# A row softmax on one core: the exponentials in a loop over a ring of 12 groups, broadcast multiplications on two engines, and one DMA queue for loads and stores

## The chip, the cores and the metric

The kernel runs on one core of one Trainium2 chip. The metric is the device time of one execution in microseconds (us), as the median of several runs. A profile is one execution more, taken by the hardware profiler, with a time of its own.

The engines that matter here are VectorE (DVE in the profile), ScalarE (ACT), GpSimd (POOL), SyncE (SP, which computes nothing and issues transfers) and the core's 16 DMA engines, which move data between the chip's memory (HBM) and the on-chip memory of 128 partitions (SBUF).

## The reference: what is computed

The input is 16 x 1024 = 16,384 rows of 512 numbers in float32. Each row is replaced by its softmax:

```python
x_max = np.max(x, axis=-1, keepdims=True)
exp_x = np.exp(x - x_max)
return (exp_x / np.sum(exp_x, axis=-1, keepdims=True)).astype(np.float32)
```

33.55 MB are read from HBM and 33.55 MB are written.

## The kernel before

**Tiles.** A chunk is 128 partitions x 16 rows x 512 numbers, which is 4 MiB; there are 8 chunks, and each is one load and one store. Partition p holds 16 consecutive rows, so that its part of a chunk is one piece of 32 KiB in HBM and in SBUF. The buffer `held` has room for 6 chunks; chunk 6 takes the place of chunk 0 and chunk 7 that of chunk 1. Everything is computed in place. The engines work on groups of 8 rows per partition, two groups to a chunk, 16 groups in all.

**One group.** `rowmax` (L86) is one VectorE reduction over 128 x 8 x 512 that gives the 8 negated row maxima (L88). `exps` (L90) is 8 ScalarE activations of 128 x 512, one for each row, with the negated maximum as bias and the row's sum as a second output (L93). `scale` (L102) is one VectorE reciprocal of the 8 sums (L104) and 8 VectorE multiplications of 128 x 512 by one number for each partition (L106).

**Order.** The main loop (L116 to L123) goes through the groups: maxima of group g, exponentials of group g, then scaling of group g-1. So VectorE alternates between a reduction and the scaling of the group before. The stores stand in the loop behind the groups that `STORE_BEHIND` names; the last ones follow it.

**Queues.** All 8 loads are issued by SyncE (L71). The first of them stands ahead of the barrier at the program's start (`loads_at_the_head`, L27), five follow at once, and loads 6 and 7 wait until stores 0 and 1 have landed, whose places they take. All 8 stores are issued by ScalarE (L74), between its activations. So loads and stores are in two DMA queues, q1 and q10 in the profile. Waits between engines are set by the framework from what each instruction reads and writes.

Of the kernel before, what the change touches and what calls it, by code (L numbers as in the profile page):

```python
# [1 line left out]

# [4 lines left out]

F32 = mybir.dt.float32
EXP = mybir.ActivationFunctionType.Exp
AX = mybir.AxisListType.X  # L10


CHUNK = 16
CHUNKS = 8
PLACES = 6
GROUP = 8

STORE_BEHIND = [1, 1, 1, 1, 0, 0, 0, 0]

LOAD_AFTER = {0: 6, 1: 7}  # L20


AT_HEAD = {mybir.EngineType.SP: 1}

def loads_at_the_head(nc):  # L27

    main, body = nc.main_func.blocks[0], nc.main_func.blocks[1]
    for engine, count in AT_HEAD.items():  # L30
        loads = [
            i
            for i in body.instructions
            if i.engine == engine and type(i).__name__ == "InstDMACopy"
        ][:count]
        barrier = next(
            n
            for n, i in enumerate(main.instructions)
            if i.engine == engine and type(i).__name__ == "InstDrain"
        )  # L40
        for load in loads:
            body.instructions.remove(load)
        main.instructions[barrier:barrier] = loads


@with_exitstack
def kernel(
    ctx: ExitStack,
    tc: tile.TileContext,
    x: bass.AP,  # L50
    out: bass.AP,
):
    nc = tc.nc
    nc.at_finalize(loads_at_the_head)
    P = nc.NUM_PARTITIONS

    x_rows = x.flatten_outer_dims().rearrange("(c p r) d -> c p r d", p=P, r=CHUNK)
    out_rows = out.flatten_outer_dims().rearrange("(c p r) d -> c p r d", p=P, r=CHUNK)
    n, _, _, d = x_rows.shape
    assert n == CHUNKS  # L60

    data = ctx.enter_context(tc.tile_pool(name="data", bufs=1))
    stats = ctx.enter_context(tc.tile_pool(name="stats", bufs=6))
    held = data.tile([P, PLACES * CHUNK, d], F32, name="held")

    def place(k):
        at = (k % PLACES) * CHUNK
        return held[:, at : at + CHUNK, :]

    def load(k):  # L70
        nc.sync.dma_start(out=place(k), in_=x_rows[k])  # L71

    def store(k):
        nc.scalar.dma_start(out=out_rows[k], in_=place(k))  # L74
        if k in LOAD_AFTER:
            load(LOAD_AFTER[k])

    per = CHUNK // GROUP
    groups = CHUNKS * per
    shift, sums = [None] * groups, [None] * groups  # L80

    def rows(g):
        at = (g % per) * GROUP
        return place(g // per)[:, at : at + GROUP, :]

    def rowmax(g):  # L86
        shift[g] = stats.tile([P, GROUP], F32, name="shift", tag="shift")
        nc.vector.reduce_max(out=shift[g], in_=rows(g), axis=AX, negate=True)  # L88

    def exps(g):  # L90
        sums[g] = stats.tile([P, GROUP], F32, name="sums", tag="sums")
        for r in range(GROUP):
            nc.scalar.activation(  # L93
                out=rows(g)[:, r, :],
                in_=rows(g)[:, r, :],
                func=EXP,
                bias=shift[g][:, r : r + 1],
                scale=1.0,
                accum_out=sums[g][:, r : r + 1],
            )  # L100

    def scale(g):  # L102
        recip = stats.tile([P, GROUP], F32, name="recip", tag="recip")
        nc.vector.reciprocal(out=recip, in_=sums[g])  # L104
        for r in range(GROUP):
            nc.vector.tensor_scalar_mul(  # L106
                out=rows(g)[:, r, :],
                in0=rows(g)[:, r, :],
                scalar1=recip[:, r : r + 1],
            )  # L110

    with tc.manual_schedule():
        for k in range(PLACES):
            load(k)
        stored = 0
        for g in range(groups):  # L116
            rowmax(g)
            exps(g)
            if g:
                scale(g - 1)  # L120
            if stored < CHUNKS and g > (stored + 1) * per - 1 + STORE_BEHIND[stored]:
                store(stored)
                stored += 1  # L123
        scale(groups - 1)
        while stored < CHUNKS:
            store(stored)
            stored += 1


# [1 line left out]
_INS = ['x']  # L131
_OUTS = [((16, 1024, 512), 'float32')]


# [23 lines left out]
```

## Time and profile before

| what | value |
|---|---|
| median of 3 runs | 161.6 us (161.31 to 162.15) |
| the profiled execution, its own time | 161.69 us |
| its span (first to last instruction) | 159.9 us |
| moved through DMA over the span | 67.1 MB, 420 GB/s |
| HBM read, written | 33.55 MB, 33.55 MB |

The profile's page has six parts: busy time by engine; the span in 40 equal slices, with the busy share of each engine and of the DMA engines in tenths; the DMA queues; the chain of work that ended last; the costliest groups of instructions, with the idle time ahead of them and what ended it; and the DMA issues. Further views are cut from the same trace: busy time and DMA rate in chosen stretches of the span, who waited for whom, and single instructions in order of time. The DMA views rest on one record for each packet that a DMA engine moved, with its start, its duration and its queue.

The span is 1.79 us shorter than the profiled execution's own time.

### The profile page before, as it was taken

The numbers are of one execution on the slowest core, as the hardware profiler recorded it, in microseconds if no ns is written. First come the engines' busy times: TensorE is split into PE (matmuls) and PEld (weight loads), VectorE is DVE, ScalarE is ACT, GpSimd is POOL, SyncE is SP. The second block draws the span as 40 slices with busy tenths as digits, with TensorE's granted clock in tenths as the row PEclk, the third lists the DMA queues.
The fourth block names the chain that finished last, engine by engine and source line by source line (L and its number), as shares of the span: only waits on it lengthen the run. The fifth ranks groups of instructions, "written<-read, shape, count | busy, mean of one in ns | idle before, by whom it ended". The sixth has DMA issues, their size and how long they took to land.

```text
span 159.9 us, 496 instructions
## 1 busy us (share of the span) xinstructions
DVE 123.5 (77%) x160; ACT 93.2 (58%) x257; POOL 0.2 (0%) x4
## 2 busy tenths in 40 slices
DVE  0008969999999999999999999999999997620000
ACT  0003799495959585867777685959594959300000
POOL 0000000000000000000000000000000000000000
DMA  8999999999999999999999999999999999999993
GB/s 270 459 443 402 451 459 402 426 469 410 402 393 393 500 412 402 467 434 410 426 459 410 418 484 404 402 500 410 402 426 484 393 410 500 402 402 500 410 402 148
DMA packets 2307, 67.13 MB, mean 420 GB/s; under 512 B 256, under 2 KB 256, under 8 KB 256
## 3 DMA queue, kind: packets, MB, share of 16 engines
q1 hardware_dynamic: 1152, 33.55, 49.5%
q10 hardware_dynamic: 1152, 33.55, 48.6%
q14 instruction: 3, 0.02, 0.0%
HBM read 33.55 MB, written 33.55 MB: 420 GB/s over the span
## 4 chain that ended last, share of the span: by engine, by line
DMA 48%; DVE 32%; ACT 8%; issue 1%; DVEq 0%; SPq 0%; ACTq 0%
DMA held<-in_x_dram 30%; DVE shift L88 19%; DMA out_dram<-held 18%; DVE held L106 12%; ACT held L93 8%; DVE recip L104 1%; DVEq L153 0%; SPq L71 0%; ACTq L93 0%
## 5 line engine op out<-in xcount | busy, mean ns | idle before, releaser
L93 ACT ACTIVATE held<-held,shift 128x512 f32<-128x512 f32 x128 | 90.5, 708 | 31.5 <-DVE shift L88 21.3
L88 DVE TENSOR_REDUCE shift<-held 128x8 f32<-128x4096 f32 x16 | 70.5, 4415 | 12.7 <-DMA held<-in_x_dram 12.7
L106 DVE TENSOR_SCALAR held<-held,recip 128x512 f32<-128x512 f32 x128 | 52.1, 482 | 0.6
L93 ACT ACTIVATION_READ_ACCUMULATOR held<-held,shift 128x1 f32 x128 | 23.9, 187 | 0.0
L93 ACT ACT_TABLE_LOAD x1 | 1.3, 1283 | 12.6 <-DMA held<-in_x_dram 12.6
L104 DVE RECIPROCAL recip<-sums 128x8 f32<-128x8 f32 x16 | 3.1, 196 | 4.0 <-ACT held L93 4.0
L142 POOL MEMSET const-bfloat16-1.0<- 128x1 bf16 x1 | 0.1, 101 | 0.0
L142 POOL MEMSET const-uint8-127<- 128x1 uint8 x1 | 0.1, 101 | 0.0
L142 POOL MEMSET const-float32-0.0<- 128x1 f32 x1 | 0.1, 98 | 0.2 <-issue 0.2
L142 POOL MEMSET const-float32-1.0<- 128x1 f32 x1 | 0.1, 98 | 0.0
## 6 DMA issues: line engine op xcount, KB each, us to landing
held<-in_x_dram SPq DMA_DIRECT2D x8, 4096.0 KB, 35.4
out_dram<-held ACTq DMA_DIRECT2D x8, 4096.0 KB, 28.4
```

Source lines behind the costliest of these rows:

```text
L88: nc.vector.reduce_max(out=shift[g], in_=rows(g), axis=AX, negate=True)
L93: nc.scalar.activation(out=rows(g)[:, r, :], in_=rows(g)[:, r, :], func=EXP, bias=shift[g][:, r : r + 1], scale=1.0, accum_out=sums[g][:, ...
L104: nc.vector.reciprocal(out=recip, in_=sums[g])
L106: nc.vector.tensor_scalar_mul(out=rows(g)[:, r, :], in0=rows(g)[:, r, :], scalar1=recip[:, r : r + 1],)
L142: nc = _bacc.Bacc("TRN2", target_bir_lowering=False, num_devices=1)
```

## The change

**Ring.** The buffer `ring` has 12 groups of 8 rows, the same bytes as 6 chunks, and is placed by hand with the statistics (`stat`: the negated maximum of a row, overwritten by its sum; `recip`). Tiles and pools are gone, and each wait is written out with a semaphore. Loads and stores still have 16 rows (two groups) and 4 MiB each, and partition p still holds 16 consecutive rows.

**ScalarE.** The 128 activations become a loop of 16 turns with 8 activations each, whose addresses are worked out in registers from `g % RING`. A turn waits for one group's maxima and signals when its 8 activations are done. ScalarE's function table is loaded ahead of the loop. It issues no DMA any more.

**VectorE.** Its order is written out in `SEQUENCE`: M is a reduction over one group, MM one over two groups, D a reciprocal and a multiplication on VectorE, P a reciprocal on VectorE and the multiplication on GpSimd. A multiplication is one instruction over 128 x 4096, with the 8 reciprocals spread along the rows (`spread`), in place of 8 instructions over 128 x 512. Groups 0, 1, 3, 5, 7, 9, 11, 13, 14 and 15 are multiplied on VectorE, groups 2, 4, 6, 8, 10 and 12 on GpSimd.

**One queue.** SyncE issues loads and stores alike: loads 0 to 5 first, as before, then the transfers in the order of `ORDER`, then store 7. A store waits until both its groups are multiplied; loads 6 and 7 wait until stores 0 and 1 have landed. What stands behind a waiting transfer on SyncE waits too.

Instructions as built: VectorE goes from 16 reductions, 16 reciprocals and 128 multiplications to 10, 16 and 10; GpSimd gets 6 multiplications; SyncE goes from 8 transfers to 16; ScalarE's program goes from 128 activations to a loop body of 8.

The diff, cut to its core (`+` is the kernel after):

```diff
-CHUNK = 16
-CHUNKS = 8
-PLACES = 6
 GROUP = 8
-STORE_BEHIND = [1, 1, 1, 1, 0, 0, 0, 0]
-LOAD_AFTER = {0: 6, 1: 7}
+RING = 12
+LOADS = [2, 2, 2, 2, 2, 2, 2, 2]
+STORES = [2, 2, 2, 2, 2, 2, 2, 2]
+ORDER = """
+S0 S1 L6 L7 S2 S3 S4 S5 S6
+"""
+SEQUENCE = """
+M0 M1 M2 D0 M3 D1 MM4 P2 MM6 D3 P4 MM8 D5 P6 MM10 D7 P8 MM12 D9 P10 MM14 D11 P12 D13 D14
+D15
+"""
...
+    ring = sbuf("ring", RING * GROUP * d)
+    stat = sbuf("stat", RING * GROUP)
+    recip = sbuf("recip", RING * GROUP)
...
     def load(k):
-        nc.sync.dma_start(out=place(k), in_=x_rows[k])
+        g, n = LOAD_AT[k], LOADS[k]
+        return nc.sync.dma_start(out=rows(g, n), in_=in_dram(x_rows, g, n))
     def store(k):
-        nc.scalar.dma_start(out=out_rows[k], in_=place(k))
-        if k in LOAD_AFTER:
-            load(LOAD_AFTER[k])
+        g, n = STORE_AT[k], STORES[k]
+        return nc.sync.dma_start(out=in_dram(out_rows, g, n), in_=rows(g, n))
...
+    def spread(t):
+        return t.unsqueeze(2).to_broadcast([P, GROUP, d])
...
+    def rowmax(g, groups):
+        nc.vector.wait_ge(loaded[load_of(g)], 16)
+        nc.vector.reduce_max(
+            out=cols(stat, g, groups), in_=rows(g, groups), axis=AX, negate=True
+        ).then_inc(maxima, groups)
+    def exps():
+        with nc.Fori(0, GROUPS, 1, engines=(ACT,)) as g:
+            nc.scalar.wait_ge(maxima, 1).then_inc(maxima, -1)
+            row = nc.scalar.snap((g % RING) * GROUP)
+            for r in range(GROUP):
+                done = exp(ring[:, bass.ds((row + r) * d, d)], stat[:, bass.ds(row + r, 1)])
+            done.then_inc(summed, 1)
+    def scale(g, engine):
+        nc.vector.wait_ge(summed, g + 1)
+        nc.vector.reciprocal(out=cols(recip, g), in_=cols(stat, g)).then_inc(inverted, 1)
+        engine.wait_ge(inverted, g + 1)
+        engine.tensor_mul(
+            out=rows(g), in0=rows(g), in1=spread(cols(recip, g))
+        ).then_inc(scaled[store_of(g)], 1)
...
+    def store_scaled(k):
+        nc.sync.wait_ge(scaled[k], STORES[k])
+        store(k).then_inc(done_by(k), 16)
+    with tc.manual_schedule(engines={ACT, DVE, POOL, SP}):
+        nc.scalar.preload_act_table(EXP)
...
+            exps()
+            for work in SEQUENCE.split():
...
+                if kind in ("M", "MM"):
+                    rowmax(g, len(kind))
+                else:
+                    scale(g, nc.vector if kind == "D" else nc.gpsimd)
+            for transfer in ORDER.split():
+                k = int(transfer[1:])
+                if transfer[0] == "S":
+                    store_scaled(k)
+                else:
...
+                    nc.sync.wait_ge(stored[last], 16 * (last - since))
+                    load(k).then_inc(loaded[k], 16)
+            nc.sync.wait_ge(scaled[-1], STORES[-1])
+        store(len(STORES) - 1)
```

## The prediction, on record before the result was known

> **What bounds the kernel now.** I read the page's busy row, the row of the DMA share, the queue rows, and then the DMA rate in stretches of the span.
>
> ```profile
> DVE 123.5 (77%) x160; ACT 93.2 (58%) x257; POOL 0.2 (0%) x4
> ...
> DMA  8999999999999999999999999999999999999993
> ...
> q1 hardware_dynamic: 1152, 33.55, 49.5%
> q10 hardware_dynamic: 1152, 33.55, 48.6%
> q14 instruction: 3, 0.02, 0.0%
> ```
>
> No engine is near 100%, but the DMA row reads 9 from the second slice to the last but one, and the two queues together take 98% of all 16 DMA engines' span. The chain of waits names DVE for 32%, but only because it steps from a store to the multiplication that released it: the transfers have other work meanwhile.
>
> The next view is the stretches (columns: stretch, length, busy time of DVE, ACT and POOL, clock, DMA share, GB/s).
>
> ```profile
> 0.00:12.50 12.50, 0.00 (x0) 0.00 (x0) 0.20 (x4) 1.00 0.94 383
> 10.00:39.90 29.90, 25.80 (x27) 19.99 (x54) 0.00 (x0) 1.00 1.01 436
> 39.90:48.00 8.10, 8.06 (x12) 6.12 (x17) 0.00 (x0) 1.00 1.00 396
> 48.00:128.00 80.00, 79.44 (x105) 59.83 (x169) 0.00 (x0) 1.00 1.00 432
> 128.00:156.00 28.00, 10.20 (x19) 7.22 (x21) 0.00 (x0) 1.00 1.00 432
> 156.00:158.00 2.00, 0.00 (x0) 0.00 (x0) 0.00 (x0) 1.00 0.69 295
> 158.00:159.90 1.90, 0.00 (x0) 0.00 (x0) 0.00 (x0) 1.00 0.00 0
> ```
>
> Until 39.9 only loads move, from 48 to 128 both directions from two queues, from 128 on only stores. The rate is 432 to 436 GB/s in all three. So a direction alone is as fast as both together, and one queue as fast as two. At 432 GB/s the 67.11 MB need 155.35 us. The span's rest is losses: 12.5 x (1 - 383/432) = 1.42 at the start; 8.1 x (1 - 396/432) = 0.68 where the first store joins the loads; 2 x (1 - 295/432) = 0.63 and 1.90 at the end. 155.35 + 1.42 + 0.68 + 0.63 + 1.90 = 159.98, against a span of 159.9. **A kernel with these transfers can win a part of 4.6 us and no more; any gap in the transfers adds its length.** All that the change does to the computing engines costs or brings nothing until a store or a load is late.
>
> **The DMA order in the kernel after.** Loads 0 to 5, stores 0 and 1, loads 6 and 7, stores 2 to 7, one after the other. 4.194 MB at 432 GB/s is 9.71 us each, and with the first loss of 1.42 the sixth load ends at 1.42 + 6 x 9.71 = 59.7. The slots then start at: S0 59.7, S1 69.4, L6 79.1, L7 88.8, S2 98.5, S3 108.2, S4 117.9, S5 127.6, S6 137.3, S7 147.0, with the end at 156.7. A store must be issued about 2 us ahead of its slot: bytes first move in the stretch from 0.5 to 1.0 after the first issue, and SP saw a landed store about 0.4 us after its last packet (83.2 to 83.7); the rest is margin.
>
> L6 needs S0 landed: 69.4 plus these 2 us is 71, and S1 occupies the engines until 79.1. L7 needs S1 landed, 81, and L6 runs until 88.8. S2 to S6 stand behind L7 on SP, so SP can't issue them before 81; S2's slot is 98.5. So the two new waits in front of stores are covered as long as S1 is issued by 67. Before, the same two waits were on SP with stores flowing in the other queue, which now can't fill a gap.
>
> **VectorE's plan.** Prices come from the groups (line, engine, operation, count | busy, mean ns | idle before).
>
> ```profile
> L93 ACT ACTIVATE held<-held,shift 128x512 f32<-128x512 f32 x128 | 90.5, 708 | 31.5 <-DVE shift L88 21.3
> L88 DVE TENSOR_REDUCE shift<-held 128x8 f32<-128x4096 f32 x16 | 70.5, 4415 | 12.7 <-DMA held<-in_x_dram 12.7
> L106 DVE TENSOR_SCALAR held<-held,recip 128x512 f32<-128x512 f32 x128 | 52.1, 482 | 0.6
> L104 DVE RECIPROCAL recip<-sums 128x8 f32<-128x8 f32 x16 | 3.1, 196 | 4.0 <-ACT held L93 4.0
> ```
>
> - M: 4.36 (4415 ns less the overlap with the next instruction; the chain has 4.33), MM twice that.
> - D, the broadcast multiplication over 128 x 4096, is in no row. Below: 3.26, what the chain shows for 8 multiplications of 512. Above: two passes of the 4415 ns row, 8.8, if the spread operand needs a pass of its own. I take 4.4, the nearest row: one instruction over the same 4096 numbers.
> - P, the same on GpSimd, is in no row; its only rows are constants of 128x1 at 98 to 101 ns. Below 4.4; above three passes of 4415 ns, 13.2. I take two passes, 8.8.
> - A reciprocal with its wait 0.2. ACT's turn: 5.76 for 8 activations (the chain: 16 pieces, 5.76). The loop's registers, wait and branch are in no row: below, nothing; above, the longest ACT wait without a seen releaser ("issue" in the waits view, 10.2 us in 5, longest 2.3) in each turn, 8.1. I take 6.0.
>
> Load 0 lands at 12.5 as before. Then M0 to 16.9, M1 21.2, M2 26.1 (load 1 lands at 21.7), D0 30.7, M3 35.1, D1 39.7, MM4 48.4, MM6 57.3, D3 61.9, MM8 70.8, D5 75.4, MM10 84.3, D7 88.9, MM12 98.4 (it waits 0.5 for load 6), D9 103.0, MM14 111.9, D11 116.5, D13 121.3, D14 125.9, D15 130.5. GpSimd starts P2 at 48.6 and has it at 57.4, P4 70.9, P6 84.4, P8 97.9, P10 112.0, P12 125.5. Stores are ready, against the need 2 us ahead of their slots: S0 39.7 (57.7), S1 61.9 (67.4), S2 75.4 (96.5), S3 88.9 (106.2), S4 103.0 (115.9), S5 116.5 (125.6), S6 125.5 (135.3), S7 130.5 (145.0). **No slot runs empty.** The tightest is S1, by 5.5 us.
>
> Other prices in the same plan tell where gaps begin. D: S5 has 9.1 us to spare and eight D ahead of it, so D over 5.6. P: six in a row from 48.6 must be done by 135.3, P over 14.4. ACT: 16 turns from 16.9 and one D by 145.0, a turn over 7.7; the 8.1 of the upper bound would cost 16 x 0.4 = 6 us. So ACT's cover is 1.9 us a turn over the row, and the loop is costed at nothing. The multiplications saved on VectorE (52.1 us busy become 44) are hidden, too.
>
> **Port rule.** Before, GpSimd does nothing beside VectorE, so no row prices the two together. If a D and a P exclude each other and M doesn't mind, the same plan has D13 wait for P12, S7 ready at 139.1, still 6 us early; but gaps begin at P over 9.8 (from 48.6, six P, five D with their reciprocal at 4.8, and the last three D, 13.6, must be done by 145.0), and then grow by 6 us for each us of P. The Trainium skill speaks against the change here: "SBUF — State Buffer", section "Who interferes with whom", says that a VectorE instruction with two SBUF inputs and a GpSimd one that reads SBUF hold the shared port in turn, the second blocked until the first is done, and that reductions are free of it. No run here shows it. "GPSIMD Engine Reference", section "Performance versus the Vector engine", has 4497 ns for 2048 columns of a two-input add; an estimate from that page is 9.0 for P, by which the sum stays the same.
>
> **What goes.** q14 is instruction loading: three packets of 8 KB in the span, at 34.5, 58.4 and 98.6 by the packet records, each holding one DMA engine for 0.31 us. At the end, 13 of 16 engines finish between 157.3 and 157.8, and three at 158.3, 158.7 and 158.8. Three packets and three late engines: that they belong together is inferred. Since the engines are never idle, a lag stays to the end. VectorE's and ScalarE's programs shrink from over 300 instructions to some 75, so most of these packets should go: between 0 and -0.97 (the last engine at 157.8 in place of 158.77); I take -0.8. On loops, "Runtime: NRT & Kernel Launch", section "Instruction fetch mechanics", warns that a jump outside the loaded window forces a fetch; the body has 21 instructions, so by that page the sum is unchanged.
>
> The loss of 0.68 where the first store joins: one queue has the change of direction three times (S0, L6, S2), but each behind transfers in the same queue. Between none (-0.68) and three like it (+1.36); I take -0.3, since the stretch from 48 to 128, with both directions mixed, shows no loss per change.
>
> Start, tail of 1.13 after the last packet, and the 1.79 around the span stay. Sum: 159.9 - 0.8 - 0.3 = 158.8 span, + 1.79 = 160.6. The profiled run's 161.69 is 0.09 above the median, so **160.5**.
>
> **Rivals.**
>
> - *Nothing is won* (the loading packets are not what makes three engines late, or every change of direction costs): 0 and +1.36 give 161.3 + 1.7 = 163.0 at the most, with one such loss as before 161.6. For it: the loss at 39.9 to 48 is real and its cause not seen. Against: the even 432. Time 161.5.
> - *GpSimd and VectorE block each other, and stores come late* (slower): it decides from P = 9.8, 1.0 above what I take. P = 10.4 adds 6 x 0.6 = 3.6 us (164.1); P = 11 7.2 (168); three passes, 13.2, 20.4 (181). S5 to S7 would be late, gaps in DMA after 127. For it: no row prices P. Against: every P starts beside an MM of 8.7 us.
> - *The broadcast multiplication costs two passes* (D = 8.8): VectorE becomes the bound, +29 us, 189. Against: it has no more numbers to write than the reduction reads.
>
> **How the numbers follow.** A difference of 0.5% (0.8 us) is about what a measurement of this kernel can tell from no change. The forecast, 159.7 to 160.8: 0.48. Nothing won, 160.8 to 162.4: 0.30. Slower 0.22: dear changes of direction up to 163.0 0.04, blocking 0.12, D or ACT dear 0.06. The low end is both gains whole, 159.9 - 0.97 - 0.68 + 1.7 = 159.95, less the 0.3 by which the fastest run stands under the median. The high end takes in the three changes of direction and blocking up to P = 10.4: 164.
>
> **What would show it.** Right: DMA share at 0.98 or more in every stretch from 2 to 155, 432 GB/s in each; fewer q14 packets, and the DMA engines done closer together; DVE ahead of its slots. Wrong: a stretch after 60 below 425 GB/s, P above 9.8 with D waiting for it, D above 5.6, ACT's turn above 7.7, or SP waiting for `scaled` with the DMA engines idle.

## The result and the profile after

| | before | after |
|---|---|---|
| median of 12 runs each, side by side | 162.05 us (161.31 to 162.69) | 161.18 us (160.97 to 161.50) |
| ratio, 95% interval | | 0.9957 (0.9942 to 0.9972) |
| profiled execution, its own time | 161.69 us | 161.16 us |
| its span | 159.9 us | 159.4 us |

The kernel after is faster by 0.43% (0.28% to 0.58%). The forecast was 160.5, a gain of 1.1 us on the median of three runs shown then. The time lies inside the range and the direction is right, but the gain was forecast too large: the ratio is worth 0.43% of 162.05, 0.7 us, and the profiled executions differ by 0.53.

The profile's page of the kernel after, the rows that answer to those of before:

```profile
DVE 121.8 (76%) x36; ACT 92.3 (58%) x257; POOL 42.3 (27%) x10
...
DMA  7999999999999999999999999999999999999993
...
q1 hardware_dynamic: 2304, 67.11, 98.4%
```

One queue now carries all 2304 packets, at the same 98% as two did. GpSimd has 42.3 us of work and ScalarE and VectorE as much as before. The row of q14, instruction loading, is gone.

The DMA rate in stretches (stretch, length, busy time of DVE, ACT and POOL, clock, DMA share, GB/s):

```profile
0.00:12.50 12.50, 0.18 (x1) 1.28 (x1) 0.20 (x4) 1.00 0.92 377
10.00:39.90 29.90, 26.57 (x9) 21.29 (x60) 0.00 (x0) 1.00 1.02 438
39.90:48.00 8.10, 8.10 (x1) 1.52 (x6) 0.00 (x0) 1.00 0.99 429
48.00:56.00 8.00, 8.00 (x3) 7.18 (x21) 7.02 (x1) 1.00 0.97 418
56.00:61.00 5.00, 4.97 (x3) 5.00 (x15) 0.00 (x0) 1.00 1.09 413
61.00:128.00 67.00, 64.58 (x20) 55.99 (x158) 35.09 (x5) 1.00 1.00 431
128.00:156.00 28.00, 9.60 (x5) 0.00 (x0) 0.00 (x0) 1.00 1.00 431
156.00:158.00 2.00, 0.00 (x0) 0.00 (x0) 0.00 (x0) 1.00 0.61 262
158.00:159.40 1.40, 0.00 (x0) 0.00 (x0) 0.00 (x0) 1.00 0.00 0
```

From 61 on the rate is an even 431, with both directions in one queue. The 396 GB/s that before had at 39.9 to 48 is now 429; the dent has moved to 56 to 61 (413), where load 5 ends and store 0 begins. There the DMA share is 1.09: the packets take longer, the queue isn't empty. A short stretch counts a packet where it starts, and 16 packets of 32 KB are 1.2 us, so that such a row shows where a dent is and not its size; the size is taken below from when transfers end. The last stretch is 1.4 us in place of 1.9.

The costliest groups (line, engine, operation, count | busy, mean ns | idle before):

```profile
L135 ACT ACTIVATE ring<-ring,stat x128 | 90.4, 707 | 31.1 <-ACTq L152 31.1
L146 DVE TENSOR_REDUCE stat<-ring 128x16 f32<-128x8192 f32 (+1 forms) x10 | 69.5, 6956 | 15.5 <-DMA ring<-in_x_dram 15.5
L162 POOL TENSOR_TENSOR ring<-ring,recip 128x4096 f32<-128x4096 f32 x6 | 42.1, 7017 | 81.7 <-DVE recip L160 81.7
L162 DVE TENSOR_TENSOR ring<-ring,recip 128x4096 f32<-128x4096 f32 x10 | 51.1, 5110 | 0.3
```

P is 7.0 us. D's mean of 5.1 mixes two prices, as the instructions in order of time show (start, duration, engine):

```profile
112.61 4.42 DVE L162 TENSOR_TENSOR ring<-ring,recip 128x4096 f32<-128x4096 f32 x1
...
117.23 7.02 POOL L162 TENSOR_TENSOR ring<-ring,recip 128x4096 f32<-128x4096 f32 x1 [6.22 <-DVE recip L160]
117.25 11.27 DVE L162 TENSOR_TENSOR ring<-ring,recip 128x4096 f32<-128x4096 f32 x1
```

Nine of the ten D take 4.42; D13 starts just behind P12 and takes 11.27, which is P12's 7.0 and its own 4.27 one after the other. D15 ends at 137.7, still ahead of store 7's slot.

SP's own waits (engine, line, releaser: us in total, times, longest):

```profile
SPq L132 <- DVE ring L162: 103.7, 6, 36.5
SPq L128 <- DMA out_dram<-ring: 18.5, 2, 9.5
```

SP spends 104 us waiting for multiplications, but the DMA row shows 9 all the while: what it waits to issue would stand in the queue anyway.

### The profile page after: what moved, and what is told of

The parts are those of the page before. It is cut to its first block, busy times and chain, and to the rows that moved or that the text cites. A ratio compares the mean times of both kernels' runs of the same rounds, so it can differ in the third digit from the quotient of the medians.

```text
span 159.4 us, 601 instructions
## 1 busy us (share of the span) xinstructions
DVE 121.8 (76%) x36; ACT 92.3 (58%) x257; POOL 42.3 (27%) x10
## 2 busy tenths in 40 slices
DMA packets 2304, 67.11 MB, mean 421 GB/s; under 512 B 256, under 2 KB 256, under 8 KB 256
## 3 DMA queue, kind: packets, MB, share of 16 engines
q1 hardware_dynamic: 2304, 67.11, 98.4%
## 4 chain that ended last, share of the span: by engine, by line
DMA 45%; DVE 39%; issue 2%; DVEq 0%
DMA ring<-in_x_dram 25%; DVE ring L162 22%; DMA out_dram<-ring 20%; DVE stat L146 16%; DVE recip L160 1%; DVEq L145 0%
## 5 line engine op out<-in xcount | busy, mean ns | idle before, releaser
L135 ACT ACTIVATE ring<-ring,stat x128 | 90.4, 707 | 31.1 <-ACTq L152 31.1
L146 DVE TENSOR_REDUCE stat<-ring 128x16 f32<-128x8192 f32 (+1 forms) x10 | 69.5, 6956 | 15.5 <-DMA ring<-in_x_dram 15.5
L162 POOL TENSOR_TENSOR ring<-ring,recip 128x4096 f32<-128x4096 f32 x6 | 42.1, 7017 | 81.7 <-DVE recip L160 81.7
L162 DVE TENSOR_TENSOR ring<-ring,recip 128x4096 f32<-128x4096 f32 x10 | 51.1, 5110 | 0.3
L135 ACT ACTIVATION_READ_ACCUMULATOR ring<-ring,stat x128 | 23.8, 186 | 0.0
L160 DVE RECIPROCAL recip<-stat 128x8 f32<-128x8 f32 x16 | 3.0, 191 | 0.0
```

Of the source, the lines that this page charges most:

```text
L135: return nc.scalar.activation(out=row, in_=row, func=EXP, bias=one, scale=1.0, accum_out=one)
L146: nc.vector.reduce_max(out=cols(stat, g, groups), in_=rows(g, groups), axis=AX, negate=True).then_inc(maxima, groups)
L160: nc.vector.reciprocal(out=cols(recip, g), in_=cols(stat, g)).then_inc(inverted, 1)
L162: engine.tensor_mul(out=rows(g), in0=rows(g), in1=spread(cols(recip, g))).then_inc(scaled[store_of(g)], 1)
```

## The experiments

Theory 1: the gain comes from instruction loading. Packets of q14 make single DMA engines late, nothing ever makes up for that, and the last engine sets the end. Theory 2: the loss at the first store is paid once in a run, whatever the queues. The rivals are told with each run. Ratios are against runs of the kernel before that were taken beside the run's own; the kernel after has 0.9957. "Last engine" is the end of the last DMA engine's last packet by the packet records, in us of the span; before has 158.8 and after 158.1. The records don't name the engine, but each engine closes each transfer with a small packet, so a transfer has 16 ends. The middle one of them is called the middle engine below, the last one the latest engine, and how far the latest is behind the middle one is its lag.

### One queue alone (b_one_queue)

```diff
-LOAD_AFTER = {0: 6, 1: 7}
+LOADS_AFTER = {1: (6, 7)}
...
 def store(k):
-    nc.scalar.dma_start(out=out_rows[k], in_=place(k))
+    nc.sync.dma_start(out=out_rows[k], in_=place(k))
...
```

> The kernel before, with its stores issued by SyncE too, in the order store 0, store 1, load 6, load 7, store 2 and so on: one queue alone. Theory 1 (instruction loading): 3 q14 packets and late engines as before, 161.7 to 162.1. Rival (two queues make engines late): the engines end within 0.8 us, 161.2. Both: the loss of about 0.8 us around the first store is there, at about 58 in place of 42, since it goes with the first store's packets and not with the number of queues.

Measured: 162.01 us, ratio 1.0010 (0.9989 to 1.0032); the page has

```profile
q1 hardware_dynamic: 2304, 67.11, 97.8%
q14 instruction: 3, 0.02, 0.0%
```

Three loading packets, and a last engine at 159.5. One queue alone brings nothing; the rival, that two queues made engines late, falls.

### The broadcast multiplications alone (b_bcast)

```diff
-for r in range(GROUP):
-    nc.vector.tensor_scalar_mul(
-        out=rows(g)[:, r, :], in0=rows(g)[:, r, :], scalar1=recip[:, r : r + 1])
+engine = nc.gpsimd if g in (2, 4, 6, 8, 10, 12) else nc.vector
+engine.tensor_mul(out=rows(g), in0=rows(g),
+                  in1=recip.unsqueeze(2).to_broadcast([P, GROUP, d]))
```

> The kernel before, with each group's 8 multiplications as one broadcast multiplication, groups 2, 4, 6, 8, 10 and 12 on GpSimd: two queues stay, VectorE's program shrinks from 161 instructions to about 43. Theory 1 (instruction loading): fewer q14 packets (1 or 2), fewer late engines, 161.4 to 161.9. Rival (two queues make engines late): three late engines as before, 162.0. Both: the last store must be issued by about 145 of the span; if VectorE ends later, as it may with GpSimd holding it up, the time grows by what is missing.

Measured: 161.38 us, ratio 0.9963 (0.9949 to 0.9977), with two queues and ScalarE written out.

```profile
q1 hardware_dynamic: 1152, 33.55, 49.7%
q10 hardware_dynamic: 1152, 33.55, 48.7%
q14 instruction: 2, 0.02, 0.0%
```

Two packets in place of three, last engine 158.4. Most of the gain comes with this part alone. But two packets are left, and the time is that of a kernel without any (a_two_queues below, 161.38 too): the number of packets alone doesn't set the time.

### ScalarE's loop undone (a_unrolled)

```diff
-with nc.Fori(0, GROUPS, 1, engines=(ACT,)) as g:
-    nc.scalar.wait_ge(maxima, 1).then_inc(maxima, -1)
-    row = nc.scalar.snap((g % RING) * GROUP)
+for g in range(GROUPS):
+    nc.scalar.wait_ge(maxima, g + 1)
+    row = at(g) * GROUP
```

> The kernel after, with ScalarE's loop written out as 128 activations (one queue, the ring and the broadcast multiplications stay). Theory 1 (instruction loading makes DMA engines late): q14 packets come back inside the span (after has none, before 3), each puts one DMA engine late by 0.3 us or more, the last engine ends some 0.5 us later than in after, and the time is 161.5 to 161.9. Rival (two queues in turn made the engines late in the kernel before, not instruction loading): packets may come back, but the 16 engines still end within 0.8 us, and the time stays at 161.2.

Measured: 162.74 us (161.72 to 163.57), ratio 1.0047 (1.0023 to 1.0071), worse than the kernel before and more than expected.

```profile
q1 hardware_dynamic: 2304, 67.11, 97.5%
q14 instruction: 2, 0.02, 0.0%
```

```profile
156.00:158.00 2.00, 0.00 (x0) 0.00 (x0) 0.00 (x0) 1.00 0.65 279
158.00:161.10 3.10, 0.00 (x0) 0.00 (x0) 0.00 (x0) 1.00 0.03 11
```

The last row shows one packet that starts after 158: the last engine is at 160.0 and the second at 158.3. The lag is 0.5 before the first packet and 0.66 after it, and goes from 0.76 to 1.44 and then 2.16 in two transfers, loads 6 and 7. Only the first of these two jumps has a loading packet in it, the one at 88.4. The second comes where load 7 ends and store 2 begins: one packet of load 7, at 98.7, took 1.92 us in place of 1.21. So about half of what the latest engine lost in these two transfers is not instruction loading. That the cost of a packet hangs on which engine it hits would fit the spread of these runs, 1.85 us against 0.53 of the kernel after; it isn't shown by itself.

### Instructions alone (a_waits and a_waits_short)

```diff
     done.then_inc(summed, 1)
+for _ in range(512):          # 1024 in a_waits
+    nc.scalar.wait_ge(loaded[0], 16)
```

> The kernel after, with 1024 waits on a semaphore that has long been reached (512 instructions) on ScalarE behind its loop, when it has nothing left to do (from about 124). No engine's work moves, and no transfer of data. Theory 1 (instruction loading): about 4 q14 packets between 110 and 155, the engines that they hit end 0.6 us later each, the time is 161.5 to 162.5. Rival (what made the longer programs slower is something else about them, such as the order or the timing of the work): 161.2.

a_waits measured: 174.72 us, ratio 1.0789 (1.0768 to 1.0809). Four packets came, at 127.3, 136.2, 146.4 and 153.8. The time doesn't answer the question: ScalarE needs some 70 ns for each of its 512 instructions, and store 7, which is issued behind the end of all engines' parts, left only at 161.3.

> The same with 512 waits (256 instructions), since with 512 instructions ScalarE was done only at about 160 (some 70 ns each) and store 7, which is issued when all engines have come to the end of their part, came 13 us late. Now ScalarE should be done at about 142, ahead of store 7's need. Theory 1: 2 q14 packets, each making one DMA engine 0.5 us late; the time goes up by 0.3 to 1.0, depending on whether they hit one engine twice or an engine that is late anyway: 161.5 to 162.2. Rival: 161.2.

a_waits_short measured: 161.85 us (161.69 to 162.08), ratio 0.9993 (0.9982 to 1.0004), 0.67 above the kernel after, or 0.6 by the two ratios.

```profile
q1 hardware_dynamic: 2304, 67.11, 98.0%
q14 instruction: 2, 0.02, 0.0%
```

Two packets at 127.1 and 137.2, last engine 158.9; nothing else has moved but store 7's issue, 2.7 us later and at 141.1 still well ahead of its slot. This takes back most of what the change had brought: the fastest of these 12 runs is slower than the slowest of the kernel after, and only instructions were added. It is the cleanest of the runs for theory 1, but its profile doesn't put all of the cost on the packets. When store 3 ends, before the first packet, the latest engine is already 0.42 behind that of the kernel after (119.70 against 119.28); it lost 0.49 at the change from load 7 to store 2, where the kernel after lost 0.13. Of the 0.77 at the end (158.88 against 158.11), 0.35 came with the packets.

### The broadcast undone on VectorE (a_rows)

```diff
-engine.tensor_mul(out=rows(g), in0=rows(g), in1=spread(cols(recip, g)))
+for r in range(GROUP):        # on VectorE; GpSimd keeps the broadcast
+    nc.vector.tensor_scalar_mul(out=rows(g)[:, r, :], in0=rows(g)[:, r, :],
+                                scalar1=cols(recip, g)[:, r : r + 1])
```

> The kernel after, with VectorE's 10 broadcast multiplications as 8 multiplications of 512 each again (80 in place of 10): VectorE's program grows to about 115 instructions, and its multiplications get cheaper (3.3 in place of 4.4 us a group). Theory: the engines' time is hidden, so the price counts for nothing; what counts is instruction loading: with no q14 packet in the span 161.2, with one 161.2 to 161.7. Rival (the broadcast form itself brings the gain): 161.6 or more without any q14 packet.

Measured: 161.44 us (161.07 to 162.18), ratio 0.9966 (0.9946 to 0.9987). VectorE is busy 110.1 us in place of 121.8, and nothing comes of it. One packet of q14 at 71.4 is in the span, last engine 158.7 in the profile. But the latest end moved by 0.13 in the transfer with that packet and by 0.60 at the change from load 7 to store 2, and the interval doesn't part this run from the kernel after; it decides nothing for theory 1.

### Loads 1 to 5 on a second queue (a_two_queues)

```diff
-return nc.sync.dma_start(out=rows(g, n), in_=in_dram(x_rows, g, n))
+engine = nc.scalar if 1 <= k < 6 else nc.sync
+return engine.dma_start(out=rows(g, n), in_=in_dram(x_rows, g, n))
```

> The kernel after, with loads 1 to 5 issued by ScalarE ahead of its loop: stores then flow in another queue beside the last loads, as in the kernel before, and the loop, the ring and the broadcast multiplications stay. If the number of queues is worth nothing (what one queue alone in the kernel before showed), no q14 packet is in the span, the engines end within 0.8 us of each other, the first store's loss is at about 42 to 45, and the time is 161.2. A rival (queues in turn cost something that the shorter programs hid): 161.5 or more.

Measured: 161.38 us, ratio 0.9966 (0.9947 to 0.9986), no loading packet of 8 KB, last engine 158.4. The 16 engines end within 0.9 us of each other, where 0.8 was expected. The number of queues is worth nothing. Load 0 shares the engines with load 1 here and is complete at about 19 in place of 12, so that computing starts 7 us later, and the time doesn't notice.

### Store 0 ahead of load 5 (a_s0_early)

```diff
-S0 S1 L6 L7 S2 S3 S4 S5 S6
+S0 L5 S1 L6 L7 S2 S3 S4 S5 S6
...
```

> The kernel after, with store 0 put ahead of load 5 in SyncE's order: five changes of direction in the queue in place of three. Theory 2 (the loss at the first store is paid once in a run): one loss of about 0.8 us, now at about 48 in place of 58, and none where load 5 follows or store 1 comes; time 161.2. Rival (each change from loads to stores, or one with many loads ahead, costs it): a second loss of 0.5 to 0.8 us near 68, time 161.7 to 162.0.

Measured: 161.50 us (161.29 to 163.67), ratio 0.9994 (0.9965 to 1.0023); two of the 12 runs took 163.0 and 163.7, which makes the interval wide, and its profiled run 161.37. The rows decide here. A transfer of 4 MiB in a full queue ends 9.68 to 9.69 after the one before it (middle DMA engine). The one ahead of store 0, now load 4, ends 10.67 after it, 0.98 late; load 5 to store 1, the second change from loads to stores, costs 0.13. For the middle engine it is paid once, then.

### Small transfers ahead of the first store

Four runs wrote 64 KB to rows of store 7 (which waits for it), from ScalarE's queue: a_touch_head and a_touch_late copy input to output within HBM, at the start and at 12.5; a_probe_early and a_probe_late store zeros from SBUF at the same places.

```diff
+nc.scalar.dma_start(out=in_dram(out_rows, GROUPS - 2, 1)[:, 0, 0:128],
+                    in_=in_dram(x_rows, 0, 1)[:, 0, 0:128]).then_inc(touched, 16)
...
+nc.scalar.dma_start(out=in_dram(out_rows, GROUPS - 2, 1)[:, 0, 0:128],
+                    in_=probe[:, :]).then_inc(touched, 16)
...
```

> The kernel after, with one transfer of 64 KB (128 x 128 numbers, from the input to rows of the output that store 7 overwrites later) issued by ScalarE at the program's start, beside load 0. Theory 2 (the loss at the first store is paid once, when this run first writes to HBM): the 0.8 us near 58 goes, or is paid beside the first loads' own late start, where part of it is hidden; the transfer itself costs about 0.2; time 160.5 to 160.9. Rival (the loss belongs to the first store behind a row of loads, or to the first read of SBUF): the 0.8 near 58 stays, time 161.2 to 161.4.

> The same transfer of 64 KB, issued by ScalarE only when load 0 has landed, at 12.5. Theory 2: a loss of 0.5 to 0.8 us moves to 13 to 15 and is gone near 58; time 161.2 to 161.4, the same as the kernel after. Rival: nothing at 13 beyond the transfer's own 0.2, the loss near 58 stays; time 161.3 to 161.5. The rows of the DMA engines' stretches tell them apart, not the time.

> The same store from SBUF, issued by ScalarE at the start, at about 2 us, while the first loads are late themselves (their first packets took 0.6 us longer than the rest). Theory 2, narrowed: the loss near 58 goes, and part of it is hidden at the start: 160.5 to 161.0. Rival A: the loss near 58 stays, 161.3 to 161.5.

> The kernel after, with a 64 KB store from SBUF (a buffer of 128 x 128 zeros, to rows of the output that store 7 overwrites later), issued by ScalarE when load 0 has landed at 12.5. Theory 2, narrowed after the copy from HBM to HBM did not take the loss away (it is paid once, when a store first reads SBUF): a loss of 0.5 to 0.8 us at 13 to 16, none near 58; time 161.2 to 161.4. Rival A (it is paid where a long row of full loads turns into full stores, whatever was stored before): none at 13 to 16, 0.7 to 0.9 near 58, time 161.3 to 161.5.

| run | median, us | ratio (interval) | load 5 behind load 4, less 9.69 |
|---|---|---|---|
| after | 161.18 | 0.9957 (0.9942 to 0.9972) | 0.64 |
| a_touch_head | 161.44 | 0.9971 (0.9958 to 0.9983) | 0.70 |
| a_touch_late | 161.45 | 0.9980 (0.9963 to 0.9997) | 0.66 |
| a_probe_early | 161.33 | 0.9963 (0.9942 to 0.9985) | 1.06 |
| a_probe_late | 161.42 | 0.9963 (0.9945 to 0.9981) | 0.81 |

None takes the loss away: neither a first write to HBM nor a first read of SBUF, when small, pays it ahead of time. Theory 2 in both of these forms falls, and the hope for a faster version with it.

### A full store early (a_copy_early)

Load 1 is followed by a store of chunk 0 as loaded to store 7's rows, and only then by loads 2 to 5; ScalarE's loop waits for it. This is 4 MiB more than the kernel moves.

```diff
...
+nc.sync.wait_ge(loaded[0], 16)
+nc.sync.dma_start(out=in_dram(out_rows, GROUPS - 2, 2), in_=rows(0, 2)).then_inc(copied, 16)
+for k in range(2, 6):
+    load(k).then_inc(loaded[k], 16)
...
```

> The kernel after, with one more full store of 4 MiB in SyncE's order behind load 1 (chunk 0 as loaded, to the rows of store 7, which overwrites them later); ScalarE's loop waits for it. It costs its own 9.7 us and some idle time while SyncE waits for load 0, so about 171 to 174. The question is where the loss of about 0.8 us at the first store is paid. If once, at the first full store: near 20, where load 1 ends, and none where store 0 follows load 5. If it belongs to a long row of loads that turns into stores: none near 20, 0.7 to 0.9 where store 0 follows. Both places: it belongs to each store that follows loads of data never touched before.

Measured: 171.26 us (two runs), ratio 1.0574 (1.0545 to 1.0604), 10.1 above the kernel after for one transfer more.

```profile
17.00:22.00 5.00, 3.99 (x1) 0.00 (x0) 0.00 (x0) 1.00 0.93 315
22.00:56.00 34.00, 21.07 (x7) 22.50 (x64) 0.00 (x0) 1.00 1.00 433
```

The dent is at 17 to 22, where load 1 ends and the full store begins: load 1 ends 10.67 after load 0, 0.98 late. Each transfer behind it ends 9.68 to 9.75 after the last (middle engine), also load 5 ahead of store 0, with four loads in a row. So the middle engine pays the loss once, where the first full store begins, and not for a long row of loads. What in the chip it is stays open.

### Without GpSimd, and with more of it (a_all_dve, a_pool_more)

```diff
-M0 M1 M2 D0 M3 D1 MM4 P2 MM6 D3 P4 MM8 D5 P6 MM10 D7 P8 MM12 D9 P10 MM14 D11 P12 D13 D14
+M0 M1 M2 D0 M3 D1 MM4 D2 MM6 D3 D4 MM8 D5 D6 MM10 D7 D8 MM12 D9 D10 MM14 D11 D12 D13 D14
```

> The kernel after, with all 16 multiplications on VectorE: this takes away what lets VectorE finish ahead of the slots of the stores. VectorE then has 16 x 4.34 + 16 x 4.42 + 16 x 0.2 us and ends at 155.4, where store 7 is wanted at 145.8; with the measured prices the plan gives 10.5 us of gaps in the transfers: 171.7. If the multiplications on GpSimd bring nothing (a rival: the covers of the plan are larger than I worked out), 161.2.

Measured: 170.39 us, ratio 1.0521 (1.0499 to 1.0544). VectorE ends at 155.7, the plan had 155.4. The transfers stand still from 118.7 and from 130.5 on, where stores 4 and 5 are late. The cover is real, and its price was 1.3 us below the forecast.

```diff
+if engine is nc.gpsimd:       # half a multiplication more, result unused
+    engine.tensor_mul(out=aside.rearrange("p (r d) -> p r d", d=d),
+                      in0=rows(g)[:, 0:4, :], in1=spread(cols(recip, g))[:, 0:4, :])
...
```

> The kernel after, with a second multiplication of 128 x 2048 on GpSimd ahead of each P, into a buffer that nothing reads: P goes from 7.0 to about 10.7 us. If VectorE's multiplications wait for GpSimd's (as D13 seems to have done in the kernel after: 11.27 in place of 4.42 us), the plan of the prediction with the measured prices gives the last stores 3.8 us late: 165.0, with D5 to D15 waiting. If they don't exclude each other, nothing is late up to P = 14.4 and the time stays at 161.2.

Measured: 162.76 us, ratio 1.0052 (1.0032 to 1.0071).

```profile
49.12 3.60 POOL L165 TENSOR_TENSOR aside<-ring,recip 128x2048 f32<-128x2048 f32 x1 [48.69 <-DVE recip L162]
52.80 7.02 POOL L171 TENSOR_TENSOR ring<-ring,recip 128x4096 f32<-128x4096 f32 x1
...
57.74 6.36 DVE L171 TENSOR_TENSOR ring<-ring,recip 128x4096 f32<-128x4096 f32 x1
...
124.97 7.86 DVE L171 TENSOR_TENSOR ring<-ring,recip 128x4096 f32<-128x4096 f32 x1
128.63 11.07 POOL L171 TENSOR_TENSOR ring<-ring,recip 128x4096 f32<-128x4096 f32 x1
```

D3, begun at 57.74, ends 4.28 after P's end at 59.82: it waits for GpSimd, while the reduction that runs beside P from 48.96 keeps its 8.63. At 124.97 D13 comes behind the first of GpSimd's two and ends before the second, which then takes 11.07: each waits for the one that came first. The plan had taken the two GpSimd instructions as one block, so the expected 165.0 is too much.

One more thing stands in this trace. It has no packet of q14 in the span, and yet its lag goes from 1.10 to 2.12 where load 7 ends and store 2 begins: the latest end moves by 1.09 us more than a transfer takes.

## Why the prediction was right in its case and wrong in its size

**DMA sets the end, and one queue is as good as two: right.** 431 in place of 432 GB/s with both directions in one queue; one queue alone 1.0010 (0.9989 to 1.0032); two queues put back, 0.9966 like the kernel after.

**No slot runs empty: right.** S1 was ready at 61.7 (plan 61.9), D15 at 137.7 (130.5, or 139.1 if D and P exclude each other), P12 at 124.3 (125.5). D was 4.42 (4.4). P was 7.0 (8.8 taken, between 4.4 and 13.2). Store 5 has seven multiplications of VectorE ahead of it and not the eight of the text, so that its bound for D was 5.7 and not 5.6; nothing hung on it. The register work of ScalarE's loop is 74 ns an activation on its own sequencer, and the activations stay at 707 ns; the loop costs the time nothing, as taken.

**Port rule: the exclusion is there, and hidden.** D13's 11.27, D3's 6.36 and GpSimd's 11.07 show it both ways round; the reductions are free of it. So these runs agree with "SBUF — State Buffer", section "Who interferes with whom", of the Trainium skill. The price of "GPSIMD Engine Reference", section "Performance versus the Vector engine", is not what this multiplication costs: 3.60 us were measured for 2048 columns where the page has 4497 ns for an add, and 7.02 for 4096, with a second input that is spread along the row. The measurement decides for this form; an add was not measured.

**Instruction loading makes engines late: right as a mechanism, its share of the gain not shown.** It was only inferred from three packets and three late engines. Now a transfer with a loading packet in it costs the 16 engines together 0.4 to 0.85 us more than the same transfer in the kernel after (ten packets in a_unrolled, a_waits, a_waits_short, a_rows and b_one_queue), and instructions alone, on an engine with nothing else to do, cost some 0.6 us. Taken -0.8; the last engine moved by -0.66 (158.77 to 158.11). But the text had loading packets as the one thing that makes engines late, and they are not. At the change from load 7 to store 2 the latest end moves by 0.04 to 1.09 us with no packet there: 1.09 in a_pool_more, 0.13 in the kernel after. In the kernel before, six packets between 62 and 85 took 0.07 to 0.21 us longer than 1.21, with the nearest loading packets at 58.4 and 98.6. How the 0.66 divides between loading and such losses stays open, and so does whether the small loss at store 2 belongs to the kernel after or to the one execution that was profiled.

The loop does here what the page "Runtime: NRT & Kernel Launch", section "Instruction fetch mechanics", allows for a target inside the loaded window: no packet in 16 turns. That section also calls the cost of loading mostly hidden; for the engine that runs the program it may be, but not in a kernel whose DMA engines are never idle.

**The first store's loss: this step failed.** The text took -0.3, "since the stretch from 48 to 128, with both directions mixed, shows no loss per change". For the middle engine that reading holds, but what follows from it is not that a part of the loss goes: it is a loss of the first full store, not of changes, and where it was measured the middle engine pays it once: 0.64 in the kernel after, 0.98 with store 0 or another full store moved ahead; a later change from loads to stores costs it 0.2 at most (a_touch_head). Measured: nothing gained in place of the 0.3. The packets between 39.5 and 62 took together 11.2 us longer than 1.213 each before and 10.6 after, which is 0.70 and 0.67 for each engine, and the middle engine ends at 157.5 in both kernels.

**The tail** I left at 1.13 after the last packet; in the profile after it is 1.27. Together: -0.66 + 0 + 0.13 is the -0.53 between the two spans, where -1.1 was forecast. For the profiled execution that is 161.16 against the 160.6 of the sum.

## What to carry to other kernels

In a kernel whose DMA engines never stand still, look at when each DMA engine ends and not only at the mean rate: 8 KB of instructions loaded in the middle of the run cost the engines more time than the 0.31 us that they take, and the whole kernel waits for the latest one. There, a shorter program (a loop, one broadcast instruction in place of eight) can be worth more than faster instructions: 12 us less work on VectorE brought nothing, and 256 idle instructions cost some 0.6 us. A late engine alone is no proof of loading, though: look in which transfer it fell behind, and whether a loading packet is in it. When a loss sits at a change of stage, move the change before you call it a loss per change.

## What was not expected of the hardware

- A loading packet takes 0.31 us of its DMA engine by its record, but its engine fell behind by about 0.5 (a_waits: from 0.40 to 0.88 and 1.42 after two of its packets). In a_unrolled an engine lost 0.7 more at 98 to 100, and in a_pool_more 1.1, without a packet there: the change from load 7 to store 2 can make single engines late. Why it does so in some executions and hardly in others is not known.
- The first full store costs 0.6 to 1.1 us on all 16 DMA engines at once, and the stall shows on the last one or two load packets ahead of it (1.3 to 2.1 us in place of 1.21).
- With loading packets in the span, runs of one kernel spread over 0.4 to 1.9 us (a_waits_short, a_unrolled); the kernel after spreads over 0.5. But kernels without a loading packet in the profiled run spread over 1.4 and 2.4 (a_touch_late, a_s0_early), so a wide spread is no sign of loading.
